# Layer 0 attention: multiplying head outputs by broadcast rows of 1/l in place of dividing the exponentials

## The chip, the cores and the metric

The kernel runs on one core of one Trainium2 chip. The metric is the device time of one execution in microseconds (us). Matmuls run on TensorE (PE in the profile, with its weight loads as PEld), element-wise work on VectorE (DVE) and ScalarE (ACT); GpSimd (POOL) and SyncE (SP) mostly start DMA transfers, each as a queue in which an instruction that waits holds up all that stand behind it.

## What is computed

A decoder trunk of two layers over 1024 tokens of width 1024, in float32. Layer 0 mixes tokens with 16 heads of width 64 side by side: heads 0 to 7 with dilated window attention (A), heads 8 to 15 with forgetting attention (B), whose logits get a bias from cumulated log forget gates. Layer 1 uses differential attention. A gated convolution network follows each mixer. What matters here is the softmax of layer 0:

```
def causal_block_probs(qb, k, q_start, bias=None):
    s = jnp.einsum('bqhd,bkhd->bhqk', qb, k, preferred_element_type=jnp.float32)
    ...
    return jax.nn.softmax(s, axis=-1)

def forgetting_attention(q, k, v, logf):
    ...
        p = causal_block_probs(qb, k, start, bias)
        return jnp.einsum('bhqk,bkhd->bqhd', p.astype(v.dtype), v)
```

The A heads come to the same form, a softmax over weighted exponentials (the kernel adds the log of how many dilation patterns hold a key), times the values, so that for both kinds of head the sum l of a query's exponentials can divide the exponentials or the output.

## The kernel before

Activations stand transposed in the chip's memory: channels on the 128 partitions, tokens along the free axis, in halves of 512. Float32 products are made of three matmuls on split operands (a rounded high part and a low part).

The attention of layer 0 is cut into 32 units, numbered in program order: for each pair of heads first half 0 with the two heads (m = 0 and 1), then half 1 with the two. Unit 15 is head 7 on half 1, unit 23 is head 11 on half 1, unit 29 is head 15 on half 0, units 30 and 31 are heads 14 and 15 on half 1. A unit has four rows of 128 queries. For a row, TensorE makes the logits (tile D), DVE adds bias or mask and takes the running minimum while it writes tile e (L590; signs are turned), ACT takes the exponential and its sum l (L681), DVE takes 1/l (L683) and multiplies the whole row of exponentials by it (L684). TensorE then transposes the row in 128x128 blocks (tile T, L148), ACT and DVE split it into ph and pl (L165, L166), and TensorE multiplies it with the values into tile O. At the unit's end ACT copies one half of O (tile rt2, L698) and DVE adds the other to it (L699), into rows 0 to 63 (m = 0) or 64 to 127 (m = 1) of tile o2. After the second head of the pair, o2 is split and stored to DRAM (od) by POOL's queue.

The function `weave` writes the events of the units in order of a slot time and puts the other matmul work of the stage between them (jobs: the projections of the later heads, then the output projection, tile pj), by costs and loads that each event carries. The builder then orders each engine's instructions itself; the order in the program's text is not the order on an engine. The job `job_load` brings the earlier heads' outputs back from od through POOL's queue, eight pairs of 256 KB at one place near unit 23 (tiles oh__ and ol__), four pairs near unit 28.

Layer 1 already has a way to spread one number per token along all partitions: `cols_to_dram` transposes a 128x4 tile by a matmul into bank "small", copies it on ACT (tile ctd) and writes it to a DRAM row; a second transfer reads the row back, broadcast to all partitions. In layer 1 both transfers go through SP's queue (tensors sr and rt) and are used in `fin_C3` (L795). The other way is `spread`: DVE multiplies the identity by a column (dg), and a matmul with ones broadcasts it.

Of the kernel before, what the change touches and what calls it, by code (L numbers as in the profile page):

```python
# [9 lines left out]
F32 = mybir.dt.float32  # L10
# [39 lines left out]
class Trunk:  # L50
# [147 lines left out]

    def cols_to_dram(self, pool, cols, w, row):

        nc = self.nc
        pt = self.small()
        self.flipped(pt[:w, :P], cols, self.ident)
        s = pool.tile([8, P], F32, name="ctd", tag="ctd", bufs=1)
        nc.scalar.activation(s[:w], pt[:w, :P], AF.Copy)
        self.put(row.rearrange("o (b q) -> (o b) q", q=P), s[:w])

# [157 lines left out]
    def job_v(self, src, n, nh, dv, dst, fg=None):  # L365


        nc = self.nc
        N = 256 + (8 if fg is not None else 0)
        idx = [self.wadd(src[:, i * 2 * N:(i + 1) * 2 * N], 2 * N) for i in range(4)]  # L370

        def gen():
            for tb in range(8):
                ps = self.pj()
                yield from self.v_mm(ps, n, idx, N, tb)
                self.v_out(ps, n, nh, dv, dst, tb)
                if fg is not None:
                    nc.vector.scalar_tensor_tensor(self.fg[:, tb * 8:tb * 8 + 8], ps[:, 256:264],
                                                   n["rc"][:, tb:tb + 1],
                                                   self.bf[:, tb * 8:tb * 8 + 8], ALU.mult, ALU.add)  # L380
            if fg is not None:
                self.forget(self.fg)
        return Job(gen, 8 * 8 * 0.33)
# [17 lines left out]

    def forget(self, z):

        nc, ap = self.nc, self.ap
        t = ap.tile([P, 64], F32, name="fg_t", bufs=1)
        lf = ap.tile([P, 64], F32, name="fg_l", bufs=1)
        nc.vector.tensor_scalar(t, z, -1.0, None, ALU.mult)
        nc.vector.tensor_tensor(t, t, z, ALU.min)
        nc.scalar.activation(t, t, AF.Exp)
        nc.scalar.activation(t, t, AF.Ln, bias=1.0)  # L410
        nc.vector.scalar_tensor_tensor(lf, z, 0.0, t, ALU.min, ALU.subtract)
        pre = ap.tile([P, 64], F32, name="fg_p", bufs=1)
        nc.gpsimd.memset(pre[:, 0:8], 0.0)
        for tb in range(1, 8):
            nc.vector.tensor_tensor(pre[:, tb * 8:tb * 8 + 8], pre[:, tb * 8 - 8:tb * 8],
                                    lf[:, tb * 8 - 8:tb * 8], ALU.add)
        ps = self.small()
        self.mm(ps[:, :64], self.tri, lf, start=True, stop=False)
        self.mm(ps[:, :64], self.ones, pre, start=False, stop=True)
        cs = t  # L420
        nc.vector.tensor_copy(cs, ps[:, :64])
        pt = self.small()
        self.flipped(pt[:64, :P], cs, self.ident)
        s = ap.tile([64, P], F32, name="fg_s", bufs=1)
        nc.scalar.activation(s, pt[:64, :P], AF.Copy)
        self.cd = self.dr.tile([8, 8, P], F32, name="cd")
        self.put(self.cd.rearrange("a b q -> (a b) q"), s)
# [215 lines left out]
    def units_AB(self, h0, qrows, krows):  # L643

        nc = self.nc
        isA = h0 < 8
        H = {}

        def mk(half, m):
            L = {"ph": {}, "e": {}}  # L650

            def load():
# [16 lines left out]
            def row(i4):  # L669
# [3 lines left out]
                def fn():  # L673
                    ap = self.ap
                    e = L["e"][i4] = ap.tile([P, T], F32, name="e", tag="e", bufs=self.ebufs)
                    st = ap.tile([P, 4], F32, name="st", tag="st", bufs=6)
                    o = 896 - i * P
                    src = self.Mt[:, o:o + W] if isA else H["nb"][m]
                    self.logits(H["k"][m], H["q", half][m], i4, W, lambda k0, w: src[:, k0:k0 + w],
                                None if isA else self.mqk, e, st[:, 0:1])  # L680
                    nc.scalar.activation(e[:, :W], e[:, :W], AF.Exp, scale=-1.0, bias=st[:, 0:1],  # L681
                                         accum_out=st[:, 1:2])
                    nc.vector.reciprocal(st[:, 2:3], st[:, 1:2])  # L683
                    nc.vector.tensor_scalar(e[:, :W], e[:, :W], st[:, 2:3], None, ALU.mult)  # L684
                return fn, 2 * W / 2266 + (0 if isA else 0.06), 1.5 * W * 0.00104 + 0.4

# [5 lines left out]
            def end(o):  # L692
# [5 lines left out]
                nc.scalar.activation(t, o[64:128], AF.Copy)  # L698
                nc.vector.tensor_tensor(o2[64 * m:64 * m + 64], o[:64], t, ALU.add)  # L699
                if m:  # L700
# [334 lines left out]
    def run(self):  # L1035
# [170 lines left out]
        self.fg = ap.tile([P, 64], F32, name="fg", bufs=1)  # L1206
        self.tri = ap.tile([P, P], F32, name="tri", bufs=1)
        self.bf = ap.tile([P, 64], F32, name="bf", bufs=1)
# [3 lines left out]
        self.put(self.Mt, a["mt"])  # L1212
        self.put(self.tri, a["tri"])
        self.put(self.bf, a["bf"].broadcast_to([P, 64]))
# [314 lines left out]
```

## Time and profile before

| | us |
|---|---|
| median of 3 runs (2620.58 to 2626.25) | 2623.19 |
| the profiled execution's own time | 2624.58 |
| its span, first to last instruction | 2622.7 |
| PE busy over the span | 2520.1 (96%) |
| DVE busy | 1873.9 (71%) |
| ACT busy | 1221.9 (47%) |
| POOL busy | 575.4 (22%) |

Layer 0's attention with the jobs woven into it runs from about 98 us to 620 us of the span. The busy shares are averages over all stages; what this change touches is read from that stretch. Times of rows below are us from the span's start.

### The profile page before, as it was taken

How to read it: one execution, taken by the hardware profiler on the slowest of the kernel's cores; microseconds unless marked ns; L12 is line 12 of the kernel's file. 1: busy time of each engine (PE TensorE's matmuls, PEld its weight loads, DVE VectorE, ACT ScalarE, POOL GpSimd, SP SyncE). 2: the span in 40 equal slices, each digit the busy share in tenths (PEclk: the TensorE clock that was granted, in tenths of full speed). 3: DMA queues.
4: the chain of work that ended last, by engine and by line, in shares of the span. 5: the costliest groups of instructions: out<-in, count | busy, mean ns of one | idle time of the engine just before them, and what ended most of it. 6: DMA issues, size and time to landing. Idle time of an engine off the chain costs nothing.

```text
span 2622.7 us, 38101 instructions
## 1 busy us (share of the span) xinstructions
PE 2520.1 (96%) x12759; PEld 2086.8 (80%) x12759; DVE 1873.9 (71%) x3721; ACT 1221.9 (47%) x2379; POOL 575.4 (22%) x730
## 2 busy tenths in 40 slices
PE   8999999999999999999999999989788999999997
PEld 7898897877678888888888888877666788888886
DVE  7788877786987665655556887868678866665564
ACT  4456655454433333544424555545444333344442
POOL 1121112232543232000011111322136432310000
PEclk9999999999999999999999999999899999999999
DMA  5655557767543222665555555776474422235563
GB/s 197 229 171 164 183 175 224 241 234 261 181 141 125 79 75 100 209 201 196 188 186 168 194 191 190 234 241 235 155 264 157 149 97 80 85 133 182 196 216 128
DMA packets 218579, 462.46 MB, mean 176 GB/s; under 512 B 33432, under 2 KB 46352, under 8 KB 218384
## 3 DMA queue, kind: packets, MB, share of 16 engines
q1 hardware_dynamic: 171728, 304.81, 36.6%
q0 software_dynamic: 46656, 155.22, 16.3%
q8 instruction: 101, 1.65, 0.3%
q14 instruction: 94, 0.77, 0.1%
HBM read 329.82 MB, written 130.08 MB: 175 GB/s over the span
## 4 chain that ended last, share of the span: by engine, by line
PE 76%; DVE 9%; DMA 6%; issue 5%; ACT 3%; POOL 1%; SPq 0%; DVEq 0%; ACTq 0%; POOLq 0%
PE pj L145 64%; PE D L145 4%; PE O L145 3%; PE T L148 3%; DMA wr<-in_wgate 2%; DVE wl L131 2%; DVE bt L166 1%; DVE v L944 1%; DVE e L590 1%; PE small L145 1%; DMA ncb<-cd 1%; ACT wh L129 1%; DMA wr<-in_woA 1%; DMA wq<-hp 1%; ACT e L739 0%
## 5 line engine op out<-in xcount | busy, mean ns | idle before, releaser
L145 PE MATMUL pj<-bt,wh 128*128 128x512 f32 x1760 | 556.9, 397 | 15.3 <-DVE bt L166 7.3
L145 PEld LDWEIGHTS pj<-bt,wh 128*128 128x128 f32 x1760 | 330.7, 189 | 100.8 <-issue 11.0
L131 DVE TENSOR_TENSOR wl<-wr,wh 128x512 fp32r<-128x512 f32 (+2 forms) x360 | 248.5, 693 | 218.2 <-ACT wh L129 209.9
L145 PE MATMUL pj<-nh,wh 128*128 128x512 f32 x864 | 357.4, 414 | 20.2 <-ACT nh L232 8.4
L129 ACT ACTIVATE wh<-wr 128x512 fp32r<-128x512 f32 (+2 forms) x360 | 223.9, 624 | 301.9 <-PE pj L145 119.9
L821 POOL TENSOR_TENSOR wq<-wq 128x512 f32<-128x512 f32 x176 | 264.8, 1505 | 388.2 <-DVE wl L131 265.5
L145 PE MATMUL pj<-bt,wl 128*128 128x512 f32 x880 | 348.4, 396 | 0.0
L145 PE MATMUL pj<-nh,wl 128*128 128x512 f32 x864 | 346.3, 401 | 0.0
L145 PE MATMUL pj<-nl,wh 128*128 128x512 f32 x864 | 346.1, 401 | 0.0
L129 ACT ACTIVATE wh<-wq 128x512 fp32r<-128x512 f32 x268 | 168.7, 630 | 359.0 <-PE pj L145 309.0
L145 PE MATMUL pj<-ah,wh 128*128 128x512 f32 (+1 forms) x716 | 280.6, 393 | 0.0
L145 PE MATMUL pj<-ah,wl 128*128 128x512 f32 (+1 forms) x716 | 279.3, 390 | 0.0
L145 PE MATMUL pj<-al,wh 128*128 128x512 f32 (+1 forms) x716 | 279.0, 390 | 0.0
L131 DVE TENSOR_TENSOR wl<-wq,wh 128x512 fp32r<-128x512 f32 x268 | 210.2, 787 | 46.5 <-ACT wh L129 46.4
L145 PEld LDWEIGHTS pj<-nh,wh 128*128 128x128 f32 x864 | 166.2, 192 | 54.9 <-ACT sc L912 14.1
L145 PEld LDWEIGHTS pj<-bt,wl 128*128 128x128 f32 x880 | 166.4, 189 | 39.3
L165 ACT ACTIVATE ph<-T 128x512 fp32r<-128x512 f32 (+3 forms) x288 | 138.8, 486 | 125.9 <-PE T L148 122.3
L145 PEld LDWEIGHTS pj<-nh,wl 128*128 128x128 f32 x864 | 165.5, 192 | 38.0 <-DVE wl L131 0.4
L145 PEld LDWEIGHTS pj<-nl,wh 128*128 128x128 f32 x864 | 166.3, 192 | 31.1 <-DVE nl L247 0.5
L166 DVE TENSOR_TENSOR pl<-T,ph 128x512 fp32r<-128x512 f32 (+3 forms) x288 | 157.4, 551 | 32.1 <-ACT ph L165 30.9
L148 PE MATMUL T<-ident,e 128*128 128x128 f32 x864 | 144.1, 277 | 20.7 <-DVE e L746 15.3
L145 PEld LDWEIGHTS pj<-ah,wl 128*128 128x128 f32 x716 | 134.4, 188 | 31.6
(460 smaller groups left out, 5060.2 us busy)
## 6 DMA issues: line engine op xcount, KB each, us to landing
wr<-in_wdown SPq DMA_DIRECT2D x176, 256.0 KB, 2.8
ar<-act SPq DMA_DIRECT2D x176, 256.0 KB, 4.4
wq<-in_wgate SPq DMA_DIRECT2D x88, 256.0 KB, 2.9
wq<-in_wup SPq DMA_DIRECT2D x88, 256.0 KB, 2.9
act<-v POOLq DMA_DIRECT2D x44, 512.0 KB, 4.3
v<-so_h POOLq DMA_DIRECT2D x64, 256.0 KB, 3.4
V<-v SPq DMA_DIRECT2D x32, 512.0 KB, 5.1
hp<-rt POOLq DMA_DIRECT2D x64, 256.0 KB, 4.0
```

The source lines that it names most:

```text
L129: nc.scalar.activation(hi[:, :n], raw[:, :n], AF.Copy)
L131: nc.vector.tensor_tensor(lo[:, :n], raw[:, :n], f(hi[:, :n]), ALU.subtract)
L145: self.last = self.nc.tensor.matmul(*args, **kw)
L148: self.last = self.nc.tensor.transpose(*args)
L165: nc.scalar.activation(hi, src, AF.Copy)
L166: nc.vector.tensor_tensor(lo, src, f(hi), ALU.subtract)
L590: self.nc.vector.tensor_tensor_reduce(out=e[:, k0:k0 + w], in0=d[:, :w], in1=in1(k0, w), scale=1.0, scalar=init, op0=ALU.add, op1=ALU.min, ...
L821: nc.gpsimd.tensor_tensor(dst, x, y, op)
L944: nc.vector.scalar_tensor_tensor(x, gt[:, j:j + T], cw[:, c0 + j:c0 + j + 1], x, ALU.mult, ALU.add)
```

## The change

The exponentials stay undivided. Each unit keeps its four sums l in one 128x4 tile; after the fourth row DVE takes all four 1/l at once (L688). In all but the last two units, `cols_to_dram` turns them into a DRAM row (lr), which is read back into half of the partitions of a new tile R (one buffer), both transfers on POOL's queue. When both heads of a pair have added their outputs, DVE multiplies o2 by R (L715). Units 30 and 31 use `spread` and multiply by its result. To make room, the causal matrix tri and the scratch tiles of `forget` share one buffer of tag rt2, and tri is fetched while the job runs. A row's load, as `weave` counts it, falls from 1.5 to 1.0 per element.

```
-    def cols_to_dram(self, pool, cols, w, row):
+    def cols_to_dram(self, pool, cols, w, row, put=None):
...
-        self.put(row.rearrange("o (b q) -> (o b) q", q=P), s[:w])
+        (put or self.put)(row.rearrange("o (b q) -> (o b) q", q=P), s[:w])
...
+                if fg is not None and tb == 6:
+                    z = self.ap.tile([P, HT], F32, name="rt2", tag="rt2", bufs=2)
+                    self.put(z[:, 320:448], self.a["tri"])
...
+        t, lf, pre, s, tri = w[:, :64], w[:, 64:128], w[:, 128:192], w[:64, 192:320], w[:, 320:448]
...
             L = {"ph": {}, "e": {}}
+            last = h0 == 14 and half == 1
...
-                    st = ap.tile([P, 4], F32, name="st", tag="st", bufs=6)
+                    st = ap.tile([P, 1], F32, name="st", tag="st", bufs=6)
+                    if i4 == 0:
+                        L["l"] = ap.tile([P, 4], F32, name="ls", tag="ls", bufs=3)
...
-                    nc.scalar.activation(e[:, :W], e[:, :W], AF.Exp, scale=-1.0, bias=st[:, 0:1],
-                                         accum_out=st[:, 1:2])
-                    nc.vector.reciprocal(st[:, 2:3], st[:, 1:2])
-                    nc.vector.tensor_scalar(e[:, :W], e[:, :W], st[:, 2:3], None, ALU.mult)
-                return fn, 2 * W / 2266 + (0 if isA else 0.06), 1.5 * W * 0.00104 + 0.4
+                    nc.scalar.activation(e[:, :W], e[:, :W], AF.Exp, scale=-1.0, bias=st,
+                                         accum_out=L["l"][:, i4:i4 + 1])
+                    if i4 == 3:
+                        nc.vector.reciprocal(L["l"], L["l"])
+                        if not last:
+                            if m == 0:
+                                H["R"] = ap.tile([P, HT], F32, name="R", tag="R", bufs=1)
+                            row = self.dr.tile([1, HT], F32, name=f"lr{h0 + m}_{half}")
+                            self.cols_to_dram(ap, L["l"], 4, row, self.store)
+                            self.store(H["R"][64 * m:64 * m + 64], row.broadcast_to([64, HT]))
+                return fn, 2 * W / 2266 + (0 if isA else 0.06), 1.0 * W * 0.00104 + 0.4
...
-                nc.vector.tensor_tensor(o2[64 * m:64 * m + 64], o[:64], t, ALU.add)
+                x = o2[64 * m:64 * m + 64]
+                nc.vector.tensor_tensor(x, o[:64], t, ALU.add)
+                if last:
+                    rp = self.spread(L["l"], ap, ("rt2", 2))
+                    nc.vector.tensor_tensor(x, x, rp[64 * m:64 * m + 64], ALU.mult)
+                elif m:
+                    nc.vector.tensor_tensor(o2, o2, H["R"], ALU.mult)
```

Two places show how the engines' orders move. The first is DVE at the end of unit 23. By then the rows of unit 24 are already under way. Before, the stretch from the division of unit 24's third row past the output add of unit 23 (L699, tile o2_5779) to unit 25's first bias step (with head 13's bias tile, ncb_5870) reads:

```order
L683 RECIPROCAL st_5903<-st_5903 128x1
L166 TENSOR_TENSOR pl_5927<-T_5924,ph_5926 128x128
L684 TENSOR_SCALAR e_5902<-e_5902,st_5903 128x384
L166 TENSOR_TENSOR so_l_5915<-rt1_5912,so_h_5914 128x512
L590 ISA e_5958,st_5959<-D_5960,ncb_5669 128x512
L590 ISA st_5959 128x1
L699 TENSOR_TENSOR o2_5779<-O_5847,rt2_5949 64x512
L166 TENSOR_TENSOR pl_5927<-T_5968,ph_5926 128x2x128
L683 RECIPROCAL st_5959<-st_5959 128x1
L590 ISA e_5973,st_5974<-D_5975,ncb_5870 128x128
```

Now it reads as follows (the add is L710, the new multiplication L715; unit 23's own 1/l, of tile ls_5639, stands 19 instructions above the multiplication):

```order
L166 TENSOR_TENSOR pl_5965<-T_5962,ph_5964 128x128
L166 TENSOR_TENSOR so_l_5945<-rt1_5942,so_h_5944 128x512
L590 ISA e_5997,st_5998<-D_5999,ncb_5707 128x512
L590 ISA st_5998 128x1
L710 TENSOR_TENSOR o2_5813<-O_5886,rt2_5987 64x512
L166 TENSOR_TENSOR pl_5965<-T_6014,ph_5964 128x2x128
L715 TENSOR_TENSOR o2_5813<-o2_5813,R_5599 128x512
L688 RECIPROCAL ls_5858<-ls_5858 128x4
L590 ISA e_6019,st_6020<-D_6022,ncb_5909 128x128
```

The divisions of each row are gone, and two instructions behind the add DVE must now have R; unit 24's four 1/l and unit 25's first bias step (tile ncb_5909) stand right behind it. The second place is POOL's queue at the same time, where the eight pairs of loads are. Before:

```order
L197 DMA oh__6125<-od00_1_96 128x512
L197 DMA ol__6126<-od01_1_104 128x512
L197 DMA oh__6129<-od00_1_96 128x512
L197 DMA ol__6130<-od01_1_104 128x512
L197 DMA oh__6133<-od00_2_97 128x512
L197 DMA ol__6134<-od01_2_105 128x512
```

Now (the third pair is oh__6171 and ol__6172, the row of unit 23 is lr11_1):

```order
L197 DMA oh__6171<-od00_1_96 128x512
L197 DMA ol__6172<-od01_1_104 128x512
L197 DMA lr11_1_5831<-ctd_5834 4x128
L197 DMA oh__6175<-od00_1_96 128x512
L197 DMA ol__6176<-od01_1_104 128x512
L197 DMA oh__6179<-od00_2_97 128x512
L197 DMA R_5599<-lr11_1_5831 64x512
L197 DMA ol__6180<-od01_2_105 128x512
L197 DMA oh__6183<-od00_2_97 128x512
```

The write of the row of 1/l now stands behind the third pair of loads, and its read behind three more loads.

## Rows read from the trace of the kernel before

**Rows 1.** Stretches: busy us of PE, PEld, DVE, ACT, POOL; PEclk, DMA share, GB/s.

```profile
98.00:620.00 522.00, 509.33 (x3190) 439.70 (x3190) 423.28 (x1113) 292.30 (x632) 112.00 (x196) 0.99 0.63 199
...
440.00:465.00 25.00, 21.50 (x127) 17.65 (x126) 18.36 (x53) 13.46 (x33) 7.84 (x15) 0.93 0.91 274
...
560.00:600.00 40.00, 35.63 (x171) 28.37 (x170) 32.48 (x71) 19.53 (x38) 11.32 (x21) 0.87 0.66 227
```

**Rows 2.** Waits of PE, 98 to 620 us: total us, times, longest.

```profile
PE T L148 <- DVE e L684: 3.8, 2, 3.4
PE D L145 <- DVE mn L590: 2.7, 2, 2.0
...
PE pj L145 <- DVE st L590: 1.1, 1, 1.1
PE small L145 <- DVE o L250: 1.1, 1, 1.1
```

**Rows 3.** Groups by line on DVE, same stretch: count | busy, mean ns | idle before.

```profile
L684 DVE TENSOR_SCALAR e<-e,st 128x384 f32<-128x384 f32 (+7 forms) x128 | 66.4, 520 | 1.9
...
L683 DVE RECIPROCAL st<-st 128x1 f32<-128x1 f32 x128 | 20.3, 159 | 23.6 <-ACT e L681 23.0
```

**Rows 4.** DVE adds of two 128x512 tiles in SBUF (L250): ns min/median/max.

```profile
L250 DVE TENSOR_TENSOR o<-o,rt x7: 677/684/694, 548.4 to 567.4; 128x512 f32<-128x512 f32 x7
```

**Rows 5.** Timeline of PE around one such transposition (small) in layer 1.

```profile
1467.65 0.39 PE L145 MATMUL pj<-nh,wl 128*128 128x512 f32 x1
1467.88 0.39 PE L145 MATMUL D<-KS,QS 128*128 128x512 f32 x1
1468.46 0.27 PE L148 MATMUL small<-ident,rq_y 128*4 128x128 f32 x1 [0.20 <-DVE rq_y L187]
1468.49 0.48 PE L145 MATMUL D<-KS,QL 128*128 128x512 f32 x1
1468.80 0.40 PE L145 MATMUL D<-KS,QS 128*128 128x512 f32 x1
```

**Rows 6.** Waits of PE in layer 1's attention, 1420 to 1880 us.

```profile
PE small L148 <- DVE rq_y L187: 1.9, 4, 1.1
```

**Rows 7.** Timeline of DVE: last division and output add of unit 29.

```profile
534.02 0.16 DVE L683 RECIPROCAL st<-st 128x1 f32<-128x1 f32 x1
...
541.26 0.68 DVE L699 TENSOR_TENSOR o<-O,rt 64x512 f32<-64x512 f32 x1
```

**Rows 8.** Timeline of SP's queue: that row's write and broadcast read in layer 1.

```profile
1469.06 0.26 SPq L194 DMA_DIRECT2D sr<-ctd  x1
...
1470.75 0.37 SPq L194 DMA_DIRECT2D rt<-sr  x1
```

**Rows 9.** Page, part 6: DMA issues of that broadcast, median us to landing.

```profile
rt<-sr SPq DMA_DIRECT2D x14, 256.0 KB, 3.1
```

**Rows 10.** Chain that ended last, layer 1, 1700 to 1722 us: start, us, what.

```profile
1700.78 7.29 DMA sr<-ctd
...
1708.09 7.60 DMA rt<-sr
```

**Rows 11.** Timeline of PE behind that chain.

```profile
1718.52 1.09 PE L148 MATMUL T<-ident,e 128*128 128x128 f32 x4 [8.04 <-DVE e L746]
```

**Rows 12.** Busy time after that gap (columns as in rows 1).

```profile
1717.00:1735.00 18.00, 16.48 (x75) 13.65 (x76) 14.70 (x39) 9.75 (x27) 8.27 (x16) 0.80 0.90 287
```

**Rows 13.** Timeline of DVE: unit 23's last division, its output add, the next bias step.

```profile
435.89 0.16 DVE L683 RECIPROCAL st<-st 128x1 f32<-128x1 f32 x1 [0.31 <-ACT e L681]
...
446.50 0.68 DVE L699 TENSOR_TENSOR o<-O,rt 64x512 f32<-64x512 f32 x1
...
450.95 0.29 DVE L590 CUSTOM_DVE_ANT_0 e<-D,ncb 128x128 f32<-128x128 f32 x1 [3.24 <-DMA ncb<-cd]
```

**Rows 14.** DMA issues on POOL's queue, 425 to 455 us: us to landing.

```profile
oh__6129<-od POOLq DMA_DIRECT2D x1, 256.0 KB, 12.8
...
ol__6142<-od POOLq DMA_DIRECT2D x1, 256.0 KB, 10.7
```

More of the change, by code (lines that the diff above doesn't have):

```diff
@@ L381, in gen @@
             if fg is not None:
-                self.forget(self.fg)
+                self.forget(self.fg, z)
         return Job(gen, 8 * 8 * 0.33)
@@ L400, in v_out, with forget @@
         self.store(self.vd[di][h0:h0 + nh, :, tb, :].rearrange("h p d -> p h d"), f(v))
[L402 to L406, printed above, removed]
+    def forget(self, z, w):
+        nc = self.nc
+        t, lf, pre, s, tri = w[:, :64], w[:, 64:128], w[:, 128:192], w[:64, 192:320], w[:, 320:448]
         nc.vector.tensor_scalar(t, z, -1.0, None, ALU.mult)
@@ L411, in forget @@
         nc.vector.scalar_tensor_tensor(lf, z, 0.0, t, ALU.min, ALU.subtract)
-        pre = ap.tile([P, 64], F32, name="fg_p", bufs=1)
         nc.gpsimd.memset(pre[:, 0:8], 0.0)
@@ L417, in forget @@
         ps = self.small()
-        self.mm(ps[:, :64], self.tri, lf, start=True, stop=False)
+        self.mm(ps[:, :64], tri, lf, start=True, stop=False)
         self.mm(ps[:, :64], self.ones, pre, start=False, stop=True)
@@ L423, in forget @@
         self.flipped(pt[:64, :P], cs, self.ident)
-        s = ap.tile([64, P], F32, name="fg_s", bufs=1)
         nc.scalar.activation(s, pt[:64, :P], AF.Copy)
@@ L679, in fn @@
                     self.logits(H["k"][m], H["q", half][m], i4, W, lambda k0, w: src[:, k0:k0 + w],
-                                None if isA else self.mqk, e, st[:, 0:1])
-                    nc.scalar.activation(e[:, :W], e[:, :W], AF.Exp, scale=-1.0, bias=st[:, 0:1],
-                                         accum_out=st[:, 1:2])
-                    nc.vector.reciprocal(st[:, 2:3], st[:, 1:2])
-                    nc.vector.tensor_scalar(e[:, :W], e[:, :W], st[:, 2:3], None, ALU.mult)
-                return fn, 2 * W / 2266 + (0 if isA else 0.06), 1.5 * W * 0.00104 + 0.4
+                                None if isA else self.mqk, e, st)
+                    nc.scalar.activation(e[:, :W], e[:, :W], AF.Exp, scale=-1.0, bias=st,
[9 more added lines that the diff above has]
+                return fn, 2 * W / 2266 + (0 if isA else 0.06), 1.0 * W * 0.00104 + 0.4
             def mms(o, v, c, ph, pl, first, last):
@@ L1206, in run @@
         self.fg = ap.tile([P, 64], F32, name="fg", bufs=1)
-        self.tri = ap.tile([P, P], F32, name="tri", bufs=1)
         self.bf = ap.tile([P, 64], F32, name="bf", bufs=1)
@@ L1212, in run @@
         self.put(self.Mt, a["mt"])
-        self.put(self.tri, a["tri"])
         self.put(self.bf, a["bf"].broadcast_to([P, 64]))
```

## The prediction

> **What bounds the kernel now.** I read the page's busy shares first (the table above), then the windows of layer 0's attention, PE's own waits there, and last the rows of the two places where the new tile R is awaited. From 98 to 620 us PE is busy for 509.3 of 522 us, DVE for 423.3, ACT for 292.3, POOL for 112.0 [rows 1]. So the stretch runs at TensorE's pace: work taken from DVE is worth only the time in which PE waited for it. PE is idle for 522 - 509.3 = 12.7 us, and the waits that the trace names for it are short: 3.8 us in front of T for the division L684, of which one wait is 3.4; 2.7 us for the running minimum; 1.1 us for the last minimum of a row; 1.1 us for the sums of the next norm [rows 2]. The one long wait is not the division's own fault: DVE stood 3.24 us for the bias tile ncb to land just before it [rows 13]. To the idle time comes a slower clock: from 440 to 465 us PE was granted 0.93 of full speed, from 560 to 600 us 0.87 [rows 1], a mean of stretches at 2.4 and at 1.2 GHz. That is 25 x 0.07 = 1.8 us and 40 x 0.13 = 5.2 us of work given away, each around idle gaps.
>
> **What goes.** DVE loses 128 row divisions and 128 reciprocals, 66.4 + 20.3 = 86.7 us, and 23.0 us of standing still for the exponentials' sums [rows 3]. It gains 32 reciprocals of 0.16 (5.1 us), 15 products of o2 and R at 0.68 as two tiles of 128x512 cost today [rows 4] (10.3 us), and for units 30 and 31 two half products and eight scalings of the identity, at most 0.68 and 0.52 each (5.5 us; bounds from the same rows). Net DVE is some 66 us lighter. Almost all of this is hidden behind PE. What PE can get back is what it waited for a late DVE: 0.4 + 2.7 + 1.1 + 1.1 = 5.3 us of rows 2 without the ncb wait, and the 5.2 us of slow clock around 560 to 600 us, where DVE was busy for 32.5 of 40 us [rows 1]. Bounds: 0 (static order, other waits come last) and 10.5 us. I take two thirds, **-7 us**, since the places are those where DVE had work queued.
>
> **What PE gets.** Thirty transpositions of the 128x4 sums and eight matmuls of `spread`. In layer 1 the same transposition starts at 1468.46, the next matmul 0.03 us later and the one after that 0.31 later, where the step between two such matmuls is 0.23 (1467.65 to 1467.88) [rows 5]: it costs 0.03 + 0.31 - 0.23 = 0.11 us. Thirty-eight make **+4.2 us**, uncovered, since PE is the bound. In front of it PE can wait for DVE: in layer 1, 1.9 us for 14 of them [rows 6], which scaled to 30 is 4.1; lower bound 0, since there the transposition comes at a pinned place and here the builder has put it behind other work. I take **+2 us**. ACT's thirty small copies and POOL's sixty issues lie on engines with 230 and 410 idle us in the stretch [rows 1]; the new weights in `weave` move jobs between rows but add none; the shared buffer for tri takes one of two rt2 buffers for some token blocks, which I put at nothing because the other buffer is free again after one copy and one add.
>
> **What the new wait costs.** DVE may not multiply o2 before R has made its way: transposition, copy, write to DRAM, its landing, read, its landing. Queued behind the multiplication on DVE are the next rows' bias steps and the pl splits, so PE stands soon after DVE does. The time allowed is from the 1/l of the pair's second head to its output add. In unit 29, the shortest of the fifteen, that is 534.18 to 541.94, 7.8 us [rows 7]. A quiet trip in layer 1 goes from the transposition at 1468.46 [rows 5] to the write at 1469.06 and the read at 1470.75 [rows 8], which by the median lands 3.1 us later [rows 9]: 5.4 us. That fits everywhere. It does not fit under load. In layer 1 one trip fell into the loads of that layer's `job_load`: the write took 7.29 us, the read 7.60 [rows 10], and PE stood 8.04 us [rows 11], followed by a granted clock of 0.80 over 18 us [rows 12], another 3.6 us.
>
> Layer 0 has the same burst at unit 23. Its 1/l is ready at 436.05, its output add ends at 447.18 [rows 13], 11.1 us later. In the changed order the row's write stands in POOL's queue behind three pairs of 256 KB loads and its read behind three loads more (the order shown with the change); loads issued at this place took 10.7 to 12.8 us to land [rows 14]. With a transposition and copy of some 2 us, the trip is 2 + 7.3 + 7.6 = 17 us by the layer 1 rows, 2 + 12.8 + 10.7 = 25 us by this queue's own. R is 6 to 14 us late. Of this, DVE stood 3.24 us anyway for ncb [rows 13], whose bias step comes right behind; what is new is 3 to 11 us, and a longer gap means a longer slow clock, up to the 3.6 - 1.8 = 1.8 us more of the layer 1 case. The floor is 0, if the write overtakes the loads. I take **+6 us**, near the lower end, since the layer 1 trip was measured on the very operation. Unit 29 comes behind the second, shorter burst with 7.8 us to go: 0 to 6 us for it and all other pairs, **+2 us**, nearer the quiet trip.
>
> The Trainium skill's page "DMA: Bandwidth & Descriptors", section "Anatomy of one DMA — SWDGE (gpsimd) path", gives a fixed cost of about 2.0 us and 436 GB/s for a transfer started by GpSimd: for 2 KB and 128 KB that makes an estimate of 2.0 + 2.3 = 4.3 us for the trip, inside every allowance, and a sum without the 6 and 2 us for late rows, -1 us. The quiet rows agree with it, the loaded ones (7.29 and 7.60) do not.
>
> **Sum.** 4.2 + 2 + 6 + 2 - 7 = +7.2 us. On the profiled execution's 2624.58 this is 2631.8; its own time stands 1.4 us over the median of the runs, 2623.19, so the median to expect is 2630.4, rounded to **2630.5 us**. A change within 0.2%, 5.2 us, can hardly be told from none in a measurement of this kernel.
>
> **Rivals.** *R comes in time everywhere.* For it speaks the quiet trip of 5.4 us; against it the one that met the burst. The sum is then 4.2 + 2 - 7 = -1, or 2622 us: no change that can be told. The Trainium skill's figure above would have it so. *DVE's lateness was the whole loss.* R comes in time, no wait in front of the transpositions, and all of the 10.5 us comes back, perhaps the 3.4 us wait and 1.8 us of clock at 451 us too because the bias tile is asked for earlier: 4.2 - 10.5 = -6.3, or 2617 us, and with the latter 2612. For it speaks that DVE is 66 us lighter where it was 81% busy; against it, that ncb is late by its own transfer. It decides from 9.4 us given back upwards (4.2 + 5.2). *The row is late by this queue's own landings*, and unit 29 and others pay too: 4.2 + 2 + 13 + 4 - 3 = +20, or 2643 us; this is the forecast's upper end.
>
> **Chances and range.** The forecast, a late R around unit 23 that outweighs what DVE gives back, slower by over 0.2%: 0.48, with its own range 2628.5 to 2645. R in time or a loss and gain that cancel, within 0.2%: 0.31. Faster by over 0.2%: 0.21. The range that leaves out no more than 2 in 10 reaches from the middle of the faster case, 2614, to 2645.
>
> **What would show it.** In the changed kernel's trace: PE's work up by 38 short matmuls; the wait of DVE at L715 for the transfer R<-lr, several us at unit 23 and near nothing in most other pairs; a PE gap there longer than the 3.4 us at 451 us, with a lower granted clock behind it; landings of the row's write and read around 440 to 455 us of 7 us and more; the waits of rows 2 for the minimum and the norm's sums gone or shorter; DVE some 66 us lighter. The prediction is wrong if no wait for R shows and PE's idle time between 98 and 620 us falls by 9 us or more, if POOL's blocked queue holds up stores of the split projections so that ACT waits for so_h, or if the order of the changed program meets waits elsewhere that I put at nothing.

## The result and the profile after

| | before | after |
|---|---|---|
| median of 4 runs each, us | 2624.72 | 2647.26 |
| the profiled execution's span, us | 2622.7 | 2647.0 |

The changed kernel takes 1.0086 times as long, with a 95% interval of 1.0073 to 1.0099: 22.6 us at 2625. The forecast was 7.2 us on the same side, and the range ended at 2645.

The windows of the kernel after, the stretches of [rows 1] with the same columns:

```profile
98.00:620.00 522.00, 497.03 (x3091) 422.45 (x3091) 356.06 (x872) 286.18 (x642) 136.88 (x244) 0.98 0.63 195
440.00:465.00 25.00, 21.84 (x142) 17.71 (x140) 14.61 (x35) 12.26 (x28) 10.85 (x21) 1.00 0.90 259
560.00:600.00 40.00, 35.73 (x179) 28.98 (x178) 27.44 (x65) 19.75 (x40) 11.31 (x21) 0.94 0.66 222
```

In these 522 us DVE is busy for 423.28 - 356.06 = 67 us less, but the stretch also holds less work now: PE ran 3091 matmuls where it ran 3190, although it had 30 more to do. At 620 us the whole program is late. What DVE lost in all is read from the whole program (part 1 of the page, before and then after):

```profile
PE 2520.1 (96%) x12759; PEld 2086.8 (80%) x12759; DVE 1873.9 (71%) x3721; ACT 1221.9 (47%) x2379; POOL 575.4 (22%) x730
```
```profile
PE 2535.2 (96%) x12805; PEld 2095.8 (79%) x12805; DVE 1828.1 (69%) x3522; ACT 1227.3 (46%) x2409; POOL 611.0 (23%) x790
```

DVE is lighter by 1873.9 - 1828.1 = 46 us, where some 66 were worked out ahead. One reason is that the forecast added up the lengths of single instructions, and neighbours overlap (below, L688 starts at 468.64 while L715 runs to 468.73). PE has 12805 - 12759 = 46 more matmuls: 30 transpositions and 16 of `spread`, of which the forecast counted 8. The waits of PE in the kernel after, against [rows 2], from 98 to 640 us (total, times, longest):

```profile
PE small L148 <- DVE ls L688: 7.6, 5, 6.4
PE T L148 <- ACT ctd L205: 5.4, 2, 4.9
PE small L145 <- DVE o L250: 2.7, 1, 2.7
PE D L145 <- DVE mn L590: 2.0, 1, 2.0
```

The wait for the division is gone, and two long ones have come, 6.4 and 4.9 us. The first is the foreseen one. POOL's queue at unit 23 shows its cause:

```profile
447.69 0.54 POOL L197 DMA_DIRECT2D ol__6172<-od  x1
449.15 0.52 POOL L197 DMA_DIRECT2D lr<-ctd  x1 [0.92 <-ACT ctd L205]
...
461.04 0.54 POOL L197 DMA_DIRECT2D R<-lr  x1 [6.26 <-DMA lr<-ctd]
```

The row's write was issued at 449.15 and landed 11.4 us later; POOL stood 6.26 us for it, and R's read came only then. DVE, the timeline at the place of [rows 13] (now the output add and the multiplication by R):

```profile
460.58 0.69 DVE L710 TENSOR_TENSOR o<-O,rt 64x512 f32<-64x512 f32 x1
...
468.04 0.69 DVE L715 TENSOR_TENSOR o<-o,R 128x512 f32<-128x512 f32 x1 [6.31 <-issue]
468.64 0.17 DVE L688 RECIPROCAL ls<-ls 128x4 f32<-128x4 f32 x1
```

The profile names no releaser for the 6.31 us, but they end when R, issued at 461.04, has landed (its longest landing, 6.9 us, is this one: 467.95). Behind the multiplication stands unit 24's own 1/l (L688), and PE's transposition of it is what PE waits for. The second long wait was not foreseen. ACT and PE, two lines of their timelines:

```profile
482.82 0.27 ACT L205 ACTIVATE ctd<-small 4x128 f32<-4x128 f32 x1 [5.71 <-DMA lr<-ctd]
...
483.14 0.90 PE L148 MATMUL T<-ident,e 128*128 128x128 f32 x3 [4.92 <-ACT ctd L205]
```

The tile ctd has one buffer. ACT may not copy the next row into it until the last row's write has landed (here 6.9 us). Bank B, one of the areas that PE writes results to, holds the transposed row until that copy and is also one of T's two banks, so PE may not make the next T. Windows show the granted clock around both (columns as in [rows 1]):

```profile
455.00:462.50 7.50, 7.21 (x48) 5.75 (x46) 4.74 (x11) 3.62 (x9) 1.46 (x3) 1.00 0.89 200
462.50:478.00 15.50, 8.84 (x45) 6.92 (x45) 6.76 (x19) 5.93 (x16) 8.80 (x17) 0.78 1.01 316
478.00:483.10 5.10, 0.22 (x1) 0.00 (x0) 1.31 (x5) 0.28 (x2) 0.62 (x2) 0.91 1.02 349
483.10:500.00 16.90, 16.86 (x77) 13.90 (x78) 8.99 (x20) 6.85 (x14) 4.26 (x8) 0.82 0.50 162
```

0.78 and 0.82 are means of time at 2.4 and at 1.2 GHz; each of the two stretches holds or follows a gap. The DMA share is 1.01 and 1.02 meanwhile: the transfer engines are full.

A third part shows in no gap of PE. Its weight loads (PEld) wait for a little many times; from 98 to 640 us, of the kernel after:

```profile
PEld small L148 <- DVE ls L688: 10.0, 11, 6.5
PEld T L148 <- ACT ctd L205: 8.8, 13, 5.4
...
PEld T L148 <- issue: 5.6, 15, 0.5
```

Compared row by row (by the start of ACT's exponential, L681 and L685), the kernel after falls back unevenly, about 0.55 us per unit in the mean: 13.2 us by the end of unit 22, long before the two gaps.

### The profile page after: what moved, and what is told of

Read it like the earlier page. It is cut to its first block, busy times and chain, and to the rows that moved or that the text cites. A ratio compares the mean times of both kernels' runs of the same rounds, so it can differ in the third digit from the quotient of the medians.

```text
span 2647.0 us, 38190 instructions
## 1 busy us (share of the span) xinstructions
PE 2535.2 (96%) x12805; PEld 2095.8 (79%) x12805; DVE 1828.1 (69%) x3522; ACT 1227.3 (46%) x2409; POOL 611.0 (23%) x790
## 4 chain that ended last, share of the span: by engine, by line
PE 78%; DVE 9%; DMA 5%; issue 4%; ACT 3%; POOL 1%; SPq 0%; DVEq 0%; ACTq 0%; POOLq 0%
PE pj L145 66%; PE D L145 4%; PE T L148 3%; PE O L145 3%; DVE wl L131 2%; DMA wr<-in_wgate 1%; DVE v L960 1%; DVE bt L166 1%; DMA lr<-ctd 1%; DVE e L590 1%; PE small L145 1%; DMA wq<-hp 1%; PE small L148 1%; ACT wh L129 1%; ACT e L755 1%
## 5 line engine op out<-in xcount | busy, mean ns | idle before, releaser
L148 PE MATMUL T<-ident,e 128*128 128x128 f32 x864 | 145.7, 280 | 21.2 <-DVE e L762 12.8
```

The source lines that it names most:

```text
L148: self.last = self.nc.tensor.transpose(*args)
```

## The experiments

All times are medians; the ratio is to the kernel before on the same chip, with its 95% interval. There are sixteen kernels. One step of the ratio of 0.001 is 2.6 us, and the intervals are 0.001 to 0.002 on either side, so a difference of two kernels is known to some 4 us.

**Taking the new path apart.** Three kernels leave out more and more of it; a fourth leaves nothing out and gives ctd three buffers in layer 0. `x1_const` multiplies o2 by ones:

```
-                    nc.vector.tensor_tensor(o2, o2, H["R"], ALU.mult)
+                    x = o2.rearrange("p (b q) -> p b q", q=P)
+                    k = self.ones.rearrange("p (a q) -> p a q", a=1).broadcast_to([P, 4, P])
+                    nc.vector.tensor_tensor(x, x, k, ALU.mult)
```

> The changed kernel, but o2 is multiplied by a tile of ones that has lain in SBUF from the start, so that nothing waits for R; the rows still go to DRAM and back into R (the heads' outputs stay undivided). Theory A (two blocks near unit 23 to 25 cost about 12 us: DVE standing for R, and ACT's copy standing for the one ctd buffer; the rest, some 13 to 16 us, is spread over all units at the transpositions): the 6.3 us wait at the multiplication goes, the ctd wait may stay: 2638 to 2643 us. Rival B (the late R, with the slow clock behind it, is nearly the whole loss): about 2627 us. Rival C (the new order of the instructions is the loss): 2645 us or more.

`x2_nodram` is x1 without the two transfers:

```
...
-    self.cols_to_dram(ap, L["l"], 4, row, self.store)
-    self.store(H["R"][64 * m:64 * m + 64], row.broadcast_to([64, HT]))
+    pt = self.small()
+    self.flipped(pt[:4, :P], L["l"], self.ident)
+    s = ap.tile([8, P], F32, name="ctd", tag="ctd", bufs=1)
+    nc.scalar.activation(s[:4], pt[:4, :P], AF.Copy)
```

> As x1_const, without both transfers: the sums are still transposed by TensorE and copied by ACT, but no row goes to DRAM and none comes back (outputs stay undivided). Theory A: both blocks gone, the cost at the transpositions left: 2630 to 2637 us. Rival B: 2624 us, as the kernel before. Rival C: 2645 us.

`x3_notrans` leaves out these four lines too.

> As x2_nodram, without the transpositions and copies either: only the reciprocals of the four sums and the product with ones are left (outputs stay undivided; units 30 and 31 keep their spread). Theory A: 13 to 16 us less than x2_nodram, 2614 to 2622 us, so a little under the kernel before, since DVE is lighter and PE was its bound. Rival B: the same as x2_nodram within 4 us. Rival C: 2640 us or more.

`y3_ctd3`:

```
...
-        s = pool.tile([8, P], F32, name="ctd", tag="ctd", bufs=1)
+        s = pool.tile([8, P], F32, name="ctd", tag="ctd", bufs=bufs)   # 3 from layer 0
```

> The changed kernel with three buffers instead of one for the copied row (ctd) in layer 0, all else as it is. Theory A: the 4.9 us wait of PE for ACT's copy near unit 25 goes, some of it comes back as later waits: 2640 to 2644 us. Rival B: 2646 us, no change that can be told.

| kernel | us | ratio | interval |
|---|---|---|---|
| x1_const | 2642.11 | 1.0059 | 1.0038 to 1.0080 |
| x2_nodram | 2631.52 | 1.0019 | 1.0010 to 1.0029 |
| x3_notrans | 2620.17 | 0.9980 | 0.9970 to 0.9991 |
| y3_ctd3 | 2637.80 | 1.0040 | 1.0025 to 1.0055 |

Without any of it the lighter DVE is worth 0.0020 x 2625 = 5.3 us. The transpositions with their copies cost 10.2 us (x2 against x3), the transfers 10.5 us although nobody waits for R (x1 against x2), and the wait for R 7.1 us more (after against x1). In x1 the foreseen gap is gone, but the one of ctd is 11.7 us long, in place of 4.9:

```profile
PE T L148 <- ACT ctd L205: 12.7, 2, 11.7
```

So the 10.5 and the 7.1 us can't be kept apart cleanly: without the one wait the other grew. Together they are 17.6 us; three buffers of ctd take 12.1 of them away and leave 5.5 (y3 against x2).

The 12.1 us of y3 are more than expected. Windows from 440 to 500 us say how much (matmuls behind PE's busy time). First before, then after:

```profile
440.00:500.00 60.00, 56.50 (x317) 46.86 (x316) 42.30 (x107) 26.15 (x57) 19.14 (x36) 0.97 0.88 276
```
```profile
440.00:500.00 60.00, 47.76 (x264) 38.53 (x263) 31.68 (x78) 25.32 (x59) 22.13 (x41) 0.89 0.82 252
```

Then x2_nodram, and y3_ctd3:

```profile
440.00:500.00 60.00, 58.34 (x343) 47.43 (x342) 40.35 (x99) 32.19 (x74) 24.80 (x46) 1.00 0.96 286
```
```profile
440.00:500.00 60.00, 55.12 (x325) 44.51 (x324) 38.84 (x94) 30.43 (x70) 25.39 (x48) 1.00 0.89 275
```

After does 264 matmuls there, y3 325: 61 more, at 60/343 = 0.17 us each some 10 us. In y3 the gap for R is left with 2.87 us, and the clock stays at 1.00.

**What in the transpositions costs.** All three are x2 with one more edit: `z2_ready` transposes four columns of a constant tile in place of the fresh 1/l, `z4_pe` is z2 without ACT's copy, `v3_copyonly` is z2 with the copy taken from a constant tile in place of the bank.

```
-    self.flipped(pt[:4, :P], L["l"], self.ident)
+    self.flipped(pt[:4, :P], self.gn[:, :4], self.ident)          # z2, z4, v3
-    nc.scalar.activation(s[:4], pt[:4, :P], AF.Copy)              # not in z4
+    nc.scalar.activation(s[:4], self.ident[:4], AF.Copy)          # v3
```

> As x2_nodram (2631.5 us), but each of the 30 transpositions takes four columns of a constant tile in place of the fresh 1/l; ACT's copy out of bank B stays, the output is multiplied by ones as in x2. Question: of what are the 11.3 us made that the transpositions cost between x3_notrans (2620.2) and x2? If PE's wait for the fresh 1/l is the larger part: 2622 to 2626, and the weight loads' wait for tile ls (5.3 us in x2) is gone. If it is the bank that small shares with T (the next T waits for ACT's copy): within 2 us of x2, 2629 to 2632, with the waits T <- ctd still there. If it is the matmuls themselves: also 2629 to 2632.

> As z2_ready, without ACT's copy: only the 30 matmuls are left of the transpositions (and the eight of the last pair), nothing waits for 1/l and nobody reads the bank. The prediction's price of the matmuls, 30 x 0.11 = 3.3 us, gives x3_notrans + 3.3 = 2623.5 (2622 to 2626). If the matmuls themselves, with the break in the stream of weights, make the 11.3 us: 2629 to 2632.

> As z2_ready (2627.1 us, ratio 0.9998), but ACT's copy takes its 4x128 elements from the constant identity in place of the bank that the matmul wrote: the same instructions on PE and ACT, and no reader holds bank B after the matmul. Between z4_pe (no copy, 2622.8, 0.9979) and z2_ready lie 5 us. If they come from the bank, held until ACT has copied while T wants it: 2621 to 2625 us, ratio about 0.998. If they come from ACT's own time, which the splits of T wait for: 2626 to 2629 us, ratio about 1.000.

| kernel | us | ratio | interval | matmuls from 98 to 400 us, less the transpositions of 1/l |
|---|---|---|---|---|
| before | | 1 | | 2040 |
| x3_notrans | 2620.17 | 0.9980 | 0.9970 to 0.9991 | 2050 |
| z4_pe | 2622.81 | 0.9979 | 0.9969 to 0.9990 | 2051 - 21 = 2030 |
| v3_copyonly | 2624.03 | 0.9988 | 0.9977 to 0.9998 | 2051 - 21 = 2030 |
| z2_ready | 2627.05 | 0.9998 | 0.9988 to 1.0008 | 2045 - 21 = 2024 |
| x2_nodram | 2631.52 | 1.0019 | 1.0010 to 1.0029 | 1998 - 20 = 1978 |
| after | 2647.26 | 1.0086 | 1.0073 to 1.0099 | 1991 - 20 = 1971 |

The last column comes from rows like these, the windows of before and x3, then that of z2 and that of x2 (the groups by line give 21 and 20 transpositions of these two):

```profile
98.00:400.00 302.00, 299.79 (x2040) 268.26 (x2040) 254.46 (x704) 181.32 (x404) 50.23 (x82) 1.00 0.55 175
```
```profile
98.00:400.00 302.00, 300.24 (x2050) 270.18 (x2049) 220.55 (x559) 180.56 (x404) 49.01 (x82) 1.00 0.58 177
```
```profile
98.00:400.00 302.00, 300.36 (x2045) 267.17 (x2044) 219.03 (x556) 182.83 (x420) 48.62 (x81) 1.00 0.58 175
```
```profile
98.00:400.00 302.00, 297.06 (x1998) 260.56 (x1998) 214.33 (x543) 178.95 (x409) 47.05 (x79) 1.00 0.55 168
```

A matmul of this stretch stands for 302 / 2050 = 0.147 us, if the mix of sizes is alike; as a check, after is (2040 - 1971) x 0.147 = 10.1 us behind before at 400 us by this count, and 8.6 to 11.9 by the rows of units 18 to 20. By that, twenty transpositions alone cost 20 x 0.147 = 2.9 us (z4 against x3), the copy 0.9, and taking the fresh 1/l 46 x 0.147 = 6.8 us, in 20 of 30 units. The rows agree. At the end of unit 22 they stand behind those of the kernel before by -1.4 us in x3, 3.6 in z4, 3.4 in v3, 4.9 in z2, 11.7 in x2 and 13.2 in after: 5.0 us for the transpositions alone, 1.3 for the copy, 6.8 for the fresh 1/l and 1.5 for the transfers, up to there. The final times say -0.2, 5.0 and 5.5 us for all 30, each to some 4 us. So the fresh 1/l is the largest part by the count and by the rows; the final times can't rank the parts. By the final time v3 lies between the two answers; by the count it equals z4, and so do its rows up to unit 22, to 0.2 us. Up to there the copy costs by the bank that it holds, 1.5 us (z2 against v3), and not by ACT's time; what the rest of its 5.0 us would be is not shown. What of the fresh 1/l can be named is time in which weight loads wait (x2, PEld, 98 to 400 us):

```profile
PEld T L148 <- issue: 4.2, 11, 0.5
PEld small L148 <- DVE ls L688: 3.2, 9, 0.6
```

z2 has 0.2 us of the first kind and none of the second. One caution: with nothing to wait for, the builder places z2's transpositions earlier on PE than x2's, by 1 to 32 matmuls, 12 in the middle. The 5.5 us are the wait together with that place.

`z3_bankA` puts x2's small into bank A, with pj:

```
-        self.bank_map(pj=["A"], small=["B"], T=["B", "U"])
+        self.bank_map(pj=["A"], small=["A"], T=["B", "U"])
```

> As x2_nodram, but in layer 0's attention the tile small lies in bank A, with the projections' tile pj, in place of bank B, which it shares with T. If the shared bank B is the larger part of the 11.3 us: 2622 to 2627 and no wait of T for ACT's copy. If it is the wait for 1/l or the matmuls: 2629 to 2632. If pj pays for the copy as T did: 2629 or more with waits of pj for ctd.

It took 2648.17 us, 1.0080 (1.0064 to 1.0097): the last case by its time, but pj's weight loads wait for ctd only 1.2 us (6 times), too little to be the cause. PE's first D of the stage waited 7.04 us for its keys' load, until 95.75 us, and by the end of unit 1 the rows are 8.1 us behind x2's; why that load came late is not shown. From unit 4 to unit 22 the rows fall back by 12.6 us (x2: 10.3) although T no longer waits for ctd, and the transpositions' weight loads wait for ls 18 times (6.9 us). So the other bank gave nothing back, but with the early gap the run is inconclusive on what bank B costs.

**Moving things in the changed kernel.** `z5_late` is y3 with the transposition and what follows it written behind the last T of the fourth row; `y2_sp` is the changed kernel with both transfers on SP's queue; `x5_weights` puts the row's load in `weave` back; `v2_pair11` is y3 with `spread` for units 22 and 23 too.

```
+            if i4 == 3 and g == half and "late" in L:       # z5, at the end of flip
+                L["late"]()                                 # transposition, copy, both transfers
...
-                            self.cols_to_dram(ap, L["l"], 4, row, self.store)
-                            self.store(H["R"][64 * m:64 * m + 64], row.broadcast_to([64, HT]))
+                            self.cols_to_dram(ap, L["l"], 4, row)                             # y2
+                            self.put(H["R"][64 * m:64 * m + 64], row.broadcast_to([64, HT]))  # y2
...
-                return fn, 2 * W / 2266 + (0 if isA else 0.06), 1.0 * W * 0.00104 + 0.4
+                return fn, 2 * W / 2266 + (0 if isA else 0.06), 1.5 * W * 0.00104 + 0.4       # x5
...
-            last = h0 == 14 and half == 1
+            last = h0 in (10, 14) and half == 1                                               # v2
```

> A correct version: y3_ctd3 (three buffers of ctd, 2637.8 us, ratio 1.004) with the transposition, its copy and both transfers written behind the transpositions of the fourth row's exponentials, in place of right behind 1/l. If PE's wait for the fresh 1/l costs what z2_ready and x2_nodram put it at (5.5 us in ratios): 2630 to 2635 us, ratio about 1.002, with the waits of small for ls near nothing. If what is won there is lost because the row is later and DVE waits for R in more pairs: 2637 to 2645.

> A correct version: the changed kernel with both transfers on SP's queue in place of POOL's, all else as it is. If the landings of 11.4 and 6.9 us at unit 23 come from POOL's queue and the loads that stand before them there: the two PE gaps near 463 and 478 us get short, 2635 to 2640 us (ratio 1.004 to 1.006). If the chip's DMA engines are simply full there, or SP's own queue now waits for the row and holds up loads: 2645 us or more.

> A correct version: the changed kernel with the row's load in weave put back from 1.0 to 1.5 per element, all else as it is. The prediction put the new weights at nothing. If so: 2644 to 2650 us (ratio 1.007 to 1.010). If the jobs that they moved are part of the loss (a projection's matmuls taken from the place where they covered a wait): 2640 or less; 2652 or more if they had helped.

> A correct version: y3_ctd3 (2637.8 us, 1.0040) with spread, as in the last pair, for heads 10 and 11 on half 1 too (units 22 and 23): no row and no R there. y3 stands 5.5 us over x2_nodram (1.0019), which has no transfers at all. If that rest is the wait for the row of unit 23 alone: 2631 to 2634 us, ratio about 1.002, and no wait of DVE for R over 1 us. If it is spread over all pairs (other transfers made slower, POOL's queue): 2637 to 2640. If spread itself costs at that place (eight scalings on DVE, bank B held by its result): 2640 or more.

| kernel | us | ratio | interval |
|---|---|---|---|
| z5_late | 2653.69 | 1.0102 | 1.0087 to 1.0117 |
| y2_sp | 2646.70 | 1.0080 | 1.0058 to 1.0101 |
| x5_weights | 2653.76 | 1.0098 | 1.0083 to 1.0113 |
| v2_pair11 | 2637.86 | 1.0034 | 1.0023 to 1.0045 |

z5 fell on the second side: the waits for ls are gone, but at unit 23 the row now starts so late that PE and DVE stand almost 16 us (timelines of PE and DVE):

```profile
480.28 0.37 PE L148 MATMUL small<-ident,ls 128*4 128x128 f32 x1 [15.89 <-DVE pl L166]
```
```profile
478.79 0.69 DVE L719 TENSOR_TENSOR o<-o,R 128x512 f32<-128x512 f32 x1 [15.82 <-issue]
```

With 16 us less it would stand at 2638, where y3 is. But DVE stands 26.5 us in all in front of this multiplication (y3: 5.9), so the run does not say what the later transposition alone is worth. y2 fell on its second side: the gap of ctd is gone (1.3 us in two waits), PE's gap for R is longer, 7.77 us, DVE waits for R again at unit 29 (3.43 us, 1.49 in after), and the time is the same. On SP's queue R's read could be issued only at 463.23 (461.04 on POOL's), after 9.3 us of waiting for the row. Whether the full transfer engines or SP's own queue, which stood 18.0 us for rows from 430 to 520 us, is the limit, the run does not tell. x5 is 0.0012 above the changed kernel, within the intervals; it gives no sign that the new weights cost anything. v2 has no long wait for R, but is 1.6 us below y3, not the 5 expected (the difference is known to some 4 us). In its place stands the bias tile that was late already in the kernel before [rows 13] (v2, DVE, then ACT and PE):

```profile
466.77 0.29 DVE L590 CUSTOM_DVE_ANT_0 e<-D,ncb 128x128 f32<-128x128 f32 x1 [4.45 <-DMA ncb<-cd]
...
467.16 0.40 ACT L685 ACTIVATE e<-e,st 128x128 f32<-128x128 f32 x1 [4.67 <-DVE st L590]
...
467.56 0.25 ACT L205 ACTIVATE ctd<-small 4x128 f32<-4x128 f32 x1
...
467.87 1.33 PE L148 MATMUL T<-ident,e 128*128 128x128 f32 x5 [4.65 <-ACT ctd L205]
```

ACT's copy stands behind the exponential that waits for that bias step, and T behind the copy. R and ncb come through the same burst, and here the kernel that has one wait taken away meets the other. In y3, where DVE waits for R, it does not wait for ncb at all.

**Other ways to the same gain.** `w2_direct` writes the row to DRAM straight from the 128x4 tile, 512 elements of 4 bytes, with no transposition and no copy; `w3_defer` is w2 with R's read at the unit's output add and the multiplication 1.2 rows later. `v1_actdiv` is the kernel before with the division on ACT, `v4_acteven` that for the first and third row of a unit only.

```
-    self.cols_to_dram(ap, L["l"], 4, row, self.store)
+    self.store(row.rearrange("o (b q) -> q (o b)", q=P), L["l"])                               # w2, w3
...
-    nc.vector.tensor_scalar(e[:, :W], e[:, :W], st[:, 2:3], None, ALU.mult)
+    nc.scalar.activation(e[:, :W], e[:, :W], AF.Copy, scale=st[:, 2:3])                        # v1, v4
```

> A correct version: the changed kernel without transposition and copy; the row of 1/l is written to DRAM straight from the 128x4 tile, as 512 elements of 4 bytes, and read back broadcast as before, on POOL's queue. Nothing new stands on PE or ACT. If the write lands in time in most units: x3_notrans plus the wait for R near unit 23, 2620 + 5 = 2622 to 2628, the same as before. If the 4-byte write is slow in every unit (over 8 us each), DVE waits for R in most of the 15 pairs: 2635 to 2660.

> A correct version, w2_direct mended in one respect: the row goes to DRAM straight from the 128x4 tile (no transposition, no copy); R's read is written at the unit's output add, and the multiplication by R and the split behind it some 1.2 rows later, so that neither POOL's queue nor DVE stands while a row lands (12.2 us in the middle in w2_direct, where POOL's queue stood 258.8 us for it). If those waits were the whole loss of w2_direct: between x3_notrans and the kernel before, 2619 to 2626 us. If the 512 elements of 4 bytes disturb other transfers, or the later output makes the last jobs late: 2632 or more.

> A correct version, from the kernel before: the division of the exponentials stays, but ACT makes it (a copy scaled by 1/l) in place of DVE; no transposition, no transfer, no R. x3_notrans showed 5.3 us for a DVE that is some 66 us lighter. If that relief can be had this way: 2618 to 2622 us, ratio 0.998, better than both kernels. If ACT, 56 percent busy in layer 0's attention and now some 70 us busier, makes T and its splits late: 2630 to 2645.

> A correct version, from the kernel before: as v1_actdiv, but only the first and third row of each unit are divided on ACT, the others on DVE as before. If relief of DVE is what counts and half of it is enough: 2619 to 2623 us. If ACT's lateness is what counts: between before and v1_actdiv.

| kernel | us | ratio | interval |
|---|---|---|---|
| w2_direct | 2764.09 | 1.0522 | 1.0498 to 1.0545 |
| w3_defer | 2770.71 | 1.0545 | 1.0528 to 1.0563 |
| v1_actdiv | 2625.90 | 0.9997 | 0.9987 to 1.0008 |
| v4_acteven | 2624.97 | 0.9994 | 0.9984 to 1.0003 |

In w2 and w3 the small elements land slowly. In w3, DMA issues from 98 to 620 us (KB each, median us to landing) and the window of that stretch:

```profile
lr<-ls POOLq DMA_DIRECT2D x27, 2.0 KB, 13.6
```
```profile
98.00:620.00 522.00, 427.45 (x2604) 372.14 (x2604) 282.42 (x714) 228.98 (x508) 113.33 (x190) 0.90 0.79 156
```

2 KB take 13.6 us, against 3.0 in the kernel after, and the transfer engines are busier (0.79 against 0.63) while they move less (156 against 195 GB/s). The Trainium skill, page "DMA: Bandwidth & Descriptors", section "Specifications", names 512 bytes as the least size for full rate, below which a transfer reads, modifies and writes; the trace agrees in direction. w3's later read did not help, POOL's queue stood 254.0 us for the row all the same (258.8 in w2, both from 98 to 620 us). How much of the loss is that queue and how much the other transfers that are slowed is not told apart. v1 and v4 make DVE 53 and 23 us lighter in that stretch (x3: 49) without any new path and gain nothing that can be told. In v1 the longest new wait is PE's for DVE's pl, 4.1 us; it stands behind the bias tile ncb, for which DVE now waits 5.93 us (3.24 before). ACT is 77 us heavier. No version beats the kernel before; only x3_notrans, which leaves the 1/l out, does.

## Why the prediction was wrong, by its own steps

The sum was 4.2 + 2 + 6 + 2 - 7 = 7.2. From the ratios, with 2625 us:

| step | predicted | measured |
|---|---|---|
| DVE's relief | -7 | -5.3 (x3) |
| matmuls of the transpositions and `spread` | +4.2 | -0.2 by the time, 2.9 for 20 of them by the count, 5.0 for 23 by the rows (z4; `spread` is in x3, so in the first row) |
| PE waits in front of the transposition | +2, at most 4.1 | +5.5 (z2 to x2) |
| ACT's copies | 0 | +5.0 by the time, 1.3 for 23 of them by the rows (z4 to z2) |
| the transfers, with nobody waiting for R | 0 | +10.5 (x2 to x1) |
| R late, at unit 23 and elsewhere | 6 + 2 | +7.1 (x1 to after) |
| sum (of the times) | 7.2 | 22.6 |

**The step that failed** is the one that put "ACT's thirty small copies and POOL's sixty issues" at nothing because they "lie on engines with 230 and 410 idle us in the stretch". By the final times it makes 15.5 us (10.5 + 5.0), as much as the 15.4 that are missing in the sum; that the other errors cancel is luck. Idle time of an engine was the wrong measure. The copy takes 0.27 us, but it holds a bank that T wants, and it needs the only buffer of ctd, which is free when the last row's write has landed. At the burst that write takes 6.9 us, ACT stands 5.71 us in front of the copy, and PE 4.92 us with a slower clock behind it. y3, with two more buffers and nothing else, gives 12.1 us back: this cause is shown, and it is the larger part of the 22.6. That the text reckoned the landing times of the same write, and asked only when R comes, not when ctd comes free, is the omission. The copy's own 5.0 us is known to some 4; the rows bear out 1.3 up to unit 22, there by the bank (v3). The prediction's last sign of being wrong, an order that "meets waits elsewhere that I put at nothing", came true.

**The wait in front of the transpositions** was scaled from layer 1 [rows 6], where PE's own waits were summed. Here most of it is no gap of PE: the weight loads wait up to 0.6 us at a time and the matmul stream thins out (1978 in place of 2024 in 302 us). The upper bound of 4.1 did not hold it by the count and by the rows, 6.8 us each; the 5.5 of the final times, known to some 4, can't tell. The ground for the lower bound, that "here the builder has put it behind other work", did not keep the weight loads from waiting for ls, 9 times from 98 to 400 us in x2. The sum also took 38 new matmuls where the trace has 46; at the prediction's own 0.11 us that is 0.9 us.

**R at unit 23** came as forecast: the write behind the loads in POOL's queue landed in 11.4 us, R in 6.9, DVE stood 6.31 us at L715 and in one other pair 1.5 us; elsewhere R was in time (3.0 us in the median for each transfer). That the 7.1 us are so near the 8 is in part luck, since they were taken with ctd's gap in place; with three buffers the transfers and R cost 5.5 together. The landings, 18.3 us in all, lie between the two prices of the prediction, 7.3 + 7.6 and 12.8 + 10.7. The Trainium skill's fit, page "DMA: Bandwidth & Descriptors", section "Anatomy of one DMA — SWDGE (gpsimd) path", would have had 2.0 us for the write, an estimate; the median of 3.0 is near it, the 11.4 is not. The write landed at 460.5 us, 0.4 us behind the load that was issued last before it (ol__6172, at 447.69, 12.4 us to landing). y2_sp shows that another queue did not make the row earlier.

**DVE's relief** was right in size, as far as it can be told: 7 lies in x3's interval, 2.4 to 7.9 us. Its place was not the forecast one. Of [rows 2] the minimum's wait falls (2.7 to 1.2 us in x3), but the one for the norm's sums grows, from 1.1 to 2.2 (after: 2.7). The clock from 440 to 465 and from 560 to 600 us, in x3, against [rows 1]:

```profile
440.00:465.00 25.00, 22.60 (x134) 17.81 (x132) 14.75 (x41) 12.78 (x31) 8.34 (x16) 1.00 0.99 290
560.00:600.00 40.00, 35.20 (x190) 28.83 (x188) 33.16 (x74) 19.60 (x38) 11.42 (x21) 0.91 0.66 217
```

Around 560 to 600 us the clock goes from 0.87 to 0.91 only. In the kernel after the 0.94 there belongs to earlier work; its own slow stretch has moved behind it (0.89 from 580 to 625 us). From 440 to 465 us the clock goes from 0.93 to 1.00, and PE's 3.41 us in front of T are 0.39, although ncb is still 2.52 us late. That was the wait which the sum had left out as ncb's. v1 and v4, which give ACT the work, gain nothing that can be told.

**The rivals.** R in time everywhere fell, by DVE's 6.31 us. DVE's lateness as the whole loss fell: x3 puts what relief brings at 5.3 us, 7.9 at most. The row late by its own queue's landings gave 2643 and came nearest, though for a reason that it had only in part: the late write also held ctd.

## What to carry to other kernels

A short instruction on an idle engine is not free when it holds something others want: list for each added instruction the bank and the buffer that it takes, and from which landing on they are free. A transfer of a few KB issued amid bulk loads should be given the loaded landing time, for its reader and for the buffer that it reads from. And on a kernel bound by TensorE a fresh operand in its stream can cost more than the gaps show (here 46 matmuls in 302 us, together with its place in the order); count the matmuls in a fixed stretch.

## What the runs showed that was not expected

PE can be 98% busy (297.06 of 302 us in x2) and still do 3.5% less work than another order of nearly the same matmuls (1978 against 2050 in x3): the loss sits in weight loads that wait, 19.3 us in x2 and 7.5 in x3 (all of PEld's waits in that stretch), mostly inside time that counts as busy. And two waits at one burst need not add up; one can take the other's place: without the wait for R, ctd's gap grew from 4.9 to 11.7 us (x1), and z2, z4 and v2 waited 4.0 to 4.5 us for ncb at the same place, x2 and y3 for neither or for R only.
